# Three queues at the start of a weight-gradient matmul: moving 384 KB from the hardware queues to the software queue

## The chip, the cores and the metric

The kernel runs on one core of a Trainium2 chip. The metric is device time in microseconds (us), the median of several executions. Of one execution the profile gives the span from the first to the last instruction (about 1.8 us less than the device time of the same execution) and a trace of every instruction and every DMA packet. Each kernel has one trace.

## The reference

```python
def setup_inputs():
    batch, m, k, n = 16, 512, 1024, 768
    return {
        "input": np.random.randn(batch, m, k).astype(np.float32),
        "grad_output": np.random.randn(batch, m, n).astype(np.float32),
    }

def reference(input, grad_output):
    return np.einsum('bmk,bmn->kn', input, grad_output).astype(np.float32)
```

Batch and m together are 8192 rows, 64 slices of 128 rows. Each slice has an X part (128 x 1024 float32, 512 KB) and a G part (128 x 768, 384 KB). The result is the sum over slices of X transposed times G.

## The kernel before

TensorE does 12 matmuls of 512 columns for each slice: eight "wide" ones (four in group A, four in group B, X as weights against the 512 wide columns of G) and four "narrow" ones (group N, the 256 narrow columns of G as weights against X). An order, tuned by hand, says which group takes which slice when, so that PSUM's eight banks and the arriving slices suffice:

```python
ORDER = (
    "A1! B1 N1 B2! N2 A2 N3! A3 B3 A4! B5 N5 B6! N7 A6 N8! A9! B10 N9 B12! N12! A12! "
    "B15 AB17! n17! AB26! n26! AB41! n41! AB47 A50! B50! N64!"
).split()
WARMUP = [512] * 10 + [128] * 2
```

"B12!" means: group B goes on up to and including the twelfth slice, then its banks are added to SBUF. Slices are counted from 0 below, so the twelfth is slice 11.

Three queues bring the inputs. GpSimd's software queue casts float32 to bf16 on the way and brings almost everything. The first slices come over the two hardware queues, SP and ACT, as float32, and DVE and ACT round them; TensorE passes the time with matmuls on constants:

```python
    xf = [head.tile([P, K], f32, name=f"xf{s}") for s in range(2)]
    gf = head.tile([P, N], f32, name="gf")
    nc.sync.dma_start(out=gf[:, 0:NA], in_=G[0:P, 0:NA])
    nc.scalar.dma_start(out=xf[0], in_=X[0:P, :])
    nc.sync.dma_start(out=gf[:, NA:N], in_=G[0:P, NA:N])
    nc.scalar.dma_start(out=xf[1], in_=X[P : 2 * P, :])
    # ... warm-up matmuls (L81) ...
    for s in range(1, S):
        gt = xg.tile([P, N], bf16, name="gt")
        nc.gpsimd.dma_start(out=gt, in_=G[s * P : (s + 1) * P, :])
        # ...
        if s > 1:
            xs[s] = xg.tile([P, K], bf16, name="xt")
            nc.gpsimd.dma_start(out=xs[s], in_=X[s * P : (s + 1) * P, :])
    # ...
    round_by("DVE", g0, gf, 0, 256)
    round_by("ACT", g0, gf, 256, NA)
    round_by("DVE", xs[0], xf[0], 0, P)
    round_by("ACT", xs[0], xf[0], 2 * P, 4 * P)
    # ... the rest of X of slice 0
```

## Time and profile before

| | kernel before |
|---|---|
| device time, median of 3 | 175.9 us |
| span of the profiled execution | 174.3 us |
| first real matmul starts | 5.32 us |
| last matmul starts | 171.25 us |
| 768 matmuls of 512 columns at 0.216 us | 165.9 us |
| X of slice 2, the first X of the software queue, lands | 9.70 us |

The lines that carry the argument stand in the prediction below.

### The profile page before, as it was taken

The numbers are of one execution on the slowest core, as the hardware profiler recorded it, in microseconds if no ns is written. First come the engines' busy times: TensorE is split into PE (matmuls) and PEld (weight loads), VectorE is DVE, ScalarE is ACT, GpSimd is POOL, SyncE is SP. The second block draws the span as 40 slices with busy tenths as digits, with TensorE's granted clock in tenths as the row PEclk, the third lists the DMA queues.
The fourth block names the chain that finished last, engine by engine and source line by source line (L and its number), as shares of the span: only waits on it lengthen the run. The fifth ranks groups of instructions, "written<-read, shape, count | busy, mean of one in ns | idle before, by whom it ended". The sixth has DMA issues, their size and how long they took to land.

```text
span 174.3 us, 2013 instructions
## 1 busy us (share of the span) xinstructions
PE 169.9 (97%) x793; PEld 78.4 (45%) x808; DVE 61.3 (35%) x103; ACT 6.2 (4%) x12; POOL 66.7 (38%) x129
## 2 busy tenths in 40 slices
PE   8999999999999999999999999999999999999993
PEld 3444444444444444444444444444444444444463
DVE  0655582883940039300000662200560003931122
ACT  2640000000000000000000000000000000000000
POOL 7444434444444444444444444444274200000000
PEclk9999999999999999999999999999999999999999
DMA  5999999999999999999999999999999990085623
GB/s 192 276 208 209 207 209 208 208 208 209 207 208 209 207 208 210 207 209 209 206 209 208 208 210 207 207 209 208 207 209 209 207 202 11 0 190 160 170 86 120
DMA packets 25048, 33.35 MB, mean 191 GB/s; under 512 B 6480, under 2 KB 16592, under 8 KB 25040
## 3 DMA queue, kind: packets, MB, share of 16 engines
q0 software_dynamic: 18000, 28.65, 89.9%
q10 hardware_dynamic: 4448, 2.10, 4.7%
q1 hardware_dynamic: 2592, 2.49, 4.2%
q8 instruction: 6, 0.10, 0.2%
q14 instruction: 2, 0.02, 0.0%
HBM read 58.72 MB, written 3.15 MB: 355 GB/s over the span
## 4 chain that ended last, share of the span: by engine, by line
PE 97%; issue 0%; DVE 0%
PE bank L127 63%; PE bank L134 32%; PE bank L81 3%; DVE acc L118 0%
## 5 line engine op out<-in xcount | busy, mean ns | idle before, releaser
L127 PE MATMUL bank<-gt,xt 128*128 128x512 bf16 (+2 forms) x515 | 108.3, 367 | 0.5
L127 PEld LDWEIGHTS <-xt 128*128 128x128 bf16 x524 | 50.2, 98 | 57.2
L118 DVE TENSOR_TENSOR acc<-bank,acc 128x512 f32<-128x512 f32 (+2 forms) x62 | 37.9, 667 | 73.4 <-PE bank L127 72.9
L134 PE MATMUL bank<-xt,gt 128*128 128x512 bf16 x242 | 54.8, 379 | 0.3
L97 POOL DMA_DIRECT2D xt<-in_input_dram x62 | 33.1, 533 | 38.7 <-DMA xt<-in_input_dram 36.5
L92 POOL DMA_DIRECT2D gt<-in_grad_output_dram x63 | 33.8, 536 | 31.2 <-DMA gt<-in_grad_output_dram 24.9
L134 PEld LDWEIGHTS <-gt 128*128 128x128 bf16 x252 | 24.6, 98 | 29.7
L118 DVE TENSOR_TENSOR acct<-bank,acct 128x512 f32<-128x512 f32 x24 | 15.7, 682 | 30.0 <-PE bank L134 29.9
L81 PE MATMUL bank<-const-bfloat16-1.0 128*128 128x512 bf16 (+1 forms) x12 | 4.6, 574 | 0.8 <-PEq L263 0.8
L81 PEld LDWEIGHTS <-const-bfloat16-1.0 128*128 128x128 bf16 x12 | 1.6, 140 | 3.5 <-issue 3.5
L122 DVE COPY acc<-bank 128x512 f32<-128x512 f32 x4 | 2.7, 687 | 1.0 <-PE bank L127 1.0
L180 DVE STREAM_TRANSPOSE turned<-acct 128x512 f32<-128x512 f32 x4 | 2.9, 715 | 0.1
L127 PEld LDWEIGHTS <-x 128*128 128x128 bf16 x16 | 1.6, 98 | 1.9 <-DVE x L107 0.2
L107 DVE CAST g<-gf 128x256 bf16<-128x256 f32 x2 | 0.6, 290 | 4.7 <-DMA gf<-in_grad_output_dram 4.7
L124 ACT COPY acc<-bank 128x512 f32<-128x512 f32 x4 | 2.1, 589 | 1.3 <-PE bank L127 1.3
L127 PE MATMUL bank<-gt,x 128*128 128x512 bf16 x8 | 2.1, 379 | 0.0
L127 PE MATMUL bank<-g,x 128*128 128x512 bf16 x8 | 2.0, 398 | 0.0
L122 DVE COPY acct<-bank 128x512 f32<-128x512 f32 x2 | 1.3, 686 | 1.3 <-PE bank L134 1.3
L107 ACT CAST x<-xf 128x256 bf16<-128x256 f32 x4 | 1.4, 409 | 0.0
L107 ACT ACT_TABLE_LOAD x1 | 1.3, 1283 | 1.7 <-PEq L263 1.7
L124 ACT COPY acct<-bank 128x512 f32<-128x512 f32 x2 | 1.1, 588 | 1.5 <-PE bank L134 1.5
L107 DVE CAST x<-xf 128x256 bf16<-128x256 f32 (+1 forms) x5 | 1.0, 260 | 0.0
(8 smaller groups left out, 3.3 us busy)
## 6 DMA issues: line engine op xcount, KB each, us to landing
xt<-in_input_dram POOLq DMA_DIRECT2D x62, 256.0 KB, 8.5
gt<-in_grad_output_dram POOLq DMA_DIRECT2D x63, 192.0 KB, 8.5
out_dram<-acc SPq DMA_DIRECT2D x13, 128.0 KB, 2.7
xf<-in_input_dram ACTq DMA_DIRECT2D x2, 512.0 KB, 5.1
out_dram<-turned ACTq DMA_DIRECT2D x4, 256.0 KB, 3.4
gf<-in_grad_output_dram SPq DMA_DIRECT2D x1, 256.0 KB, 3.9
out_dram<-acc SPq DMA_DIRECT2D x1, 256.0 KB, 2.0
gf<-in_grad_output_dram SPq DMA_DIRECT2D x1, 128.0 KB, 4.7
```

What stands on the lines that cost most here:

```text
L81: nc.tensor.matmul(wps[:, 0:cols], ones, nc.const_aps.tensor(1.0, (P, cols), bf16), start=True, stop=True,)
L92: nc.gpsimd.dma_start(out=gt, in_=G[s * P : (s + 1) * P, :])
L97: nc.gpsimd.dma_start(out=xs[s], in_=X[s * P : (s + 1) * P, :])
L107: copy(out=dst[:, c0:c1], in_=src[:, c0:c1])
L118: nc.vector.tensor_add(out=dst, in0=src, in1=dst)
L122: nc.vector.tensor_copy(out=dst, in_=src)
L124: nc.scalar.copy(out=dst, in_=src)
L127: nc.tensor.matmul(bank, xs[s][:, k * P : (k + 1) * P], gwide[s][:, c0:c1], start=start, stop=stop)
L134: nc.tensor.matmul(bank, gnarrow[s].rearrange("p (r t) -> p t r", t=NT)[:, t], xs[s][:, h * NA : (h + 1) * NA], start=start, stop=stop,)
L180: nc.vector.transpose(out=turned[:, h * hb : (h + 1) * hb, :, t], in_=dst.rearrange("p (b r) -> p b r", r=SQ),)
```

## The change

Its intent: give TensorE its first data sooner. Wide G and the first half of X of slice 0 lead the two hardware queues in equal 2 KB rows, the warm-up is shortened to match, and 384 KB that are needed a little later (narrow G of slice 0, the low half of X of slice 1) go to the software queue, which also saves their rounding.

```diff
-WARMUP = [512] * 10 + [128] * 2
+WARMUP = [512] * 9 + [128] * 3
...
-    nc.sync.dma_start(out=gf[:, 0:NA], in_=G[0:P, 0:NA])
-    nc.scalar.dma_start(out=xf[0], in_=X[0:P, :])
-    nc.sync.dma_start(out=gf[:, NA:N], in_=G[0:P, NA:N])
-    nc.scalar.dma_start(out=xf[1], in_=X[P : 2 * P, :])
+    nc.sync.dma_start(out=gf, in_=G[0:P, 0:NA])
+    nc.scalar.dma_start(out=xf[0][:, 0:NA], in_=X[0:P, 0:NA])
+    nc.sync.dma_start(out=xf[1][:, NA:K], in_=X[P : 2 * P, NA:K])
+    nc.scalar.dma_start(out=xf[0][:, NA:K], in_=X[0:P, NA:K])
...
-    for s in range(1, S):
+    for s in range(S):
...
+        g0 = NA if s == 0 else 0
+        nc.gpsimd.dma_start(out=gt[:, g0:N], in_=G[s * P : (s + 1) * P, g0:N])
+        if s > 0:
+            x1 = NA if s == 1 else K
+            nc.gpsimd.dma_start(out=xs[s][:, 0:x1], in_=X[s * P : (s + 1) * P, 0:x1])
...
-    round_by("DVE", g0, gf, 0, 256)
-    round_by("ACT", g0, gf, 256, NA)
+    round_by("DVE", gwide[0], gf, 0, 304)
+    round_by("ACT", gwide[0], gf, 304, NA)
... (X of slice 0 is rounded in pieces of 128, then 256 columns; narrow G of slice 0
...  and the low half of X of slice 1 are no longer rounded)
-        "N": Part(narrow_mm, [(t, h) for h in range(KH) for t in range(NT)], narrow_dst),
+        "N": Part(narrow_mm, [(t, h) for h in reversed(range(KH)) for t in range(NT)], narrow_dst),
```

More of the change, by code (lines that the diff above doesn't have):

```diff
@@ L70 @@
     xf = [head.tile([P, K], f32, name=f"xf{s}") for s in range(2)]
-    gf = head.tile([P, N], f32, name="gf")
-    nc.sync.dma_start(out=gf[:, 0:NA], in_=G[0:P, 0:NA])
-    nc.scalar.dma_start(out=xf[0], in_=X[0:P, :])
-    nc.sync.dma_start(out=gf[:, NA:N], in_=G[0:P, NA:N])
-    nc.scalar.dma_start(out=xf[1], in_=X[P : 2 * P, :])
+    gf = head.tile([P, NA], f32, name="gf")
+    nc.sync.dma_start(out=gf, in_=G[0:P, 0:NA])
+    nc.scalar.dma_start(out=xf[0][:, 0:NA], in_=X[0:P, 0:NA])
+    nc.sync.dma_start(out=xf[1][:, NA:K], in_=X[P : 2 * P, NA:K])
+    nc.scalar.dma_start(out=xf[0][:, NA:K], in_=X[0:P, NA:K])
     ones = nc.const_aps.tensor(1.0, (P, P), bf16)
@@ L87 @@
         )
-    for s in range(1, S):
-        gt = xg.tile([P, N], bf16, name="gt")
-        nc.gpsimd.dma_start(out=gt, in_=G[s * P : (s + 1) * P, :])
+    for s in range(S):
+        pool = head if s == 0 else xg
+        gt = pool.tile([P, N], bf16, name="gt")
+        pool = head if s < 2 else xg
+        xs[s] = pool.tile([P, K], bf16, name=f"x{s}" if s < 2 else "xt")
         gwide[s] = gt[:, 0:NA]
         gnarrow[s] = gt[:, NA:N]
-        if s > 1:
-            xs[s] = xg.tile([P, K], bf16, name="xt")
-            nc.gpsimd.dma_start(out=xs[s], in_=X[s * P : (s + 1) * P, :])
-    for s in range(2):
-        xs[s] = head.tile([P, K], bf16, name=f"x{s}")
-    g0 = head.tile([P, N], bf16, name="g0")
-    gwide[0] = g0[:, 0:NA]
-    gnarrow[0] = g0[:, NA:N]
+        g0 = NA if s == 0 else 0
[3 more added lines that the diff above has]
+            nc.gpsimd.dma_start(out=xs[s][:, 0:x1], in_=X[s * P : (s + 1) * P, 0:x1])
     def round_by(engine, dst, src, c0, c1):
@@ L107, in round_by @@
         copy(out=dst[:, c0:c1], in_=src[:, c0:c1])
-    round_by("DVE", g0, gf, 0, 256)
-    round_by("ACT", g0, gf, 256, NA)
-    round_by("DVE", xs[0], xf[0], 0, P)
-    round_by("ACT", xs[0], xf[0], 2 * P, 4 * P)
-    round_by("DVE", xs[0], xf[0], P, 2 * P)
-    round_by("DVE", xs[0], xf[0], 4 * P, 6 * P)
-    round_by("ACT", xs[0], xf[0], 6 * P, 8 * P)
+    round_by("DVE", gwide[0], gf, 0, 304)
+    round_by("ACT", gwide[0], gf, 304, NA)
+    for k in range(0, KS // 2, 2):
+        round_by("DVE", xs[0], xf[0], k * P, (k + 1) * P)
+        round_by("ACT", xs[0], xf[0], (k + 1) * P, (k + 2) * P)
+    round_by("DVE", xs[0], xf[0], NA, 6 * P)
+    round_by("ACT", xs[0], xf[0], 6 * P, K)
     def add_out(dst, src):
@@ L172, in add_slice @@
             copy_out(dst, bank, i)
-            if s == 0 and i == 0:
-                round_by("DVE", g0, gf, NA, N)
         else:
@@ L212 @@
     for i, step in enumerate(ORDER):
-        if i == 2:
-            round_by("DVE", xs[1], xf[1], 4 * P, 6 * P)
-            round_by("ACT", xs[1], xf[1], 6 * P, 8 * P)
-            round_by("DVE", xs[1], xf[1], 0, 2 * P)
-            round_by("ACT", xs[1], xf[1], 2 * P, 4 * P)
+        if i == 1:
+            round_by("DVE", xs[1], xf[1], NA, 6 * P)
+            round_by("ACT", xs[1], xf[1], 6 * P, K)
         close = step.endswith("!")
```

## The prediction

> **What bounds the kernel now.** I read the page first, for what the end of the span hangs on.
>
> ```profile
> ## 4 chain that ended last, share of the span: by engine, by line
> PE 97%; issue 0%; DVE 0%
> PE bank L127 63%; PE bank L134 32%; PE bank L81 3%; DVE acc L118 0%
> ```
>
> The chain is TensorE from end to end: wide matmuls (L127), narrow ones (L134), and 3% of warm-up matmuls on constants (L81). No wait holds even 1%. So the time is: when the real matmuls start, plus their number times their spacing, plus every gap in them, plus the tail. There are 64 slices of 12 matmuls of 512 columns, 768 in all. The chain puts groups of four 0.86 us apart, so 0.216 us each and 768 x 0.216 = 165.9 us. The timeline has the first real one at 5.32 and the last addition from PSUM starting at 171.50, which leaves no room for gaps. The change touches neither count nor tail, only the first 5.3 us and the arrivals of early slices. So next I read the timeline of the start (start, duration, then the wait in brackets).
>
> ```profile
> 0.78 4.64 PE L81 MATMUL bank<-const-bfloat16-1.0 128*128 128x512 bf16 x12 [0.78 <-PEq L263]
> ...
> 1.23 1.20 POOL L92 DMA_DIRECT2D gt<-in_grad_output_dram  x2 [0.79 <-POOLq L263]
> ...
> 4.71 0.29 DVE L107 CAST g<-gf 128x256 bf16<-128x256 f32 x1 [4.71 <-DMA gf<-in_grad_output_dram]
> ...
> 5.04 0.56 DVE L107 CAST x<-xf 128x128 bf16<-128x128 f32 x3
> ...
> 5.32 1.55 PEld L127 LDWEIGHTS <-x 128*128 128x128 bf16 x8 [0.17 <-DVE x L107]
> 5.32 2.04 PE L127 MATMUL bank<-g,x 128*128 128x512 bf16 x8
> ```
>
> The reader sees a chain G of slice 0 landed (4.7), X of slice 0 landed (5.0), rounded, first real weights at 5.32, with TensorE waiting 0.17 us for the rounding. The warm-up fills the time until then. Asked over narrow windows, the timeline puts the warm-up matmuls 0.427 us apart, the first real one at 5.32, the second at 5.69 and then one each 0.216: the array ran at half rate until within the first real matmul. Solving 0.362 us = one matmul, part at 0.427 and part at 0.216 per matmul, puts the switch near 5.6. (The granted clock in the page reads full all along; the spacing is the witness.)
>
> Third, the DMA view of two adjoining windows, 4.5 to 5.25 and 5 to 5.5. In the first the software queue has no row at all; in the second it appears:
>
> ```profile
> q10 hardware_dynamic: 64, 0.25, 83.7%
> q1 hardware_dynamic: 69, 0.06, 22.1%
> ...
> q10 hardware_dynamic: 46, 0.19, 94.2%
> q0 software_dynamic: 5, 0.01, 8.4%
> q1 hardware_dynamic: 16, 0.00, 3.6%
> ```
>
> The software queue, first issued at 1.23, moves nothing until about 5.25, when the SP queue (q1) runs dry. From then to 145 us the transfers are saturated at about 208 GB/s. So the third question is how early each slice lands before its first use. I took issue time plus landing time per transfer and set it against the matmul rows. The tightest is X of slice 11:
>
> ```profile
> L97 POOL DMA_DIRECT2D xt<-in_input_dram x1: 530/530/530, 21.0 to 21.0; - x1
> DMA to landing us min/median/max: 9.2/9.2/9.2
> ...
> 29.64 1.89 PE L127 MATMUL bank<-gt,xt 128*128 128x512 bf16 x8
> ```
>
> It lands at about 30.15; the fifth matmul of that row needs it at 29.64 + 4 x 0.216 = 30.50. **Margin about 0.35 us.** Other margins, got likewise: slice 16 0.55, slice 1 0.57, slice 6 0.77, slice 4 0.87, slice 2 0.95; late slices over 1.3. Slice 11 is tight because of an instruction fetch (q8, 16 KB at about 24 us) that occupies one DMA engine for 0.9 us.
>
> **What the Trainium skill says.** "TensorE: Matmul & The Clock Gate", What's actually happening: the array starts at half clock, and a free-running activity window of about 3.4 us decides when it is released, so it is a budget of time and not of matmuls. The 0.427 to 0.216 us step agrees. If so, less warm-up does not bring the switch forward. "DMA: Bandwidth & Descriptors", Queues, rings and completion order: each DMA engine goes round the queues that have work, a packet at a time. Agrees for the two hardware queues: between 3 and 5 us q10 with 4 KB rows moved 0.57 MB and q1 with rows of 2 KB and less 0.25 MB, so the longer row takes the larger share. The same page, Latency and other measured facts, has first byte of a software transfer at about 1 us; this trace has 4 us, and the measurement decides. The same page, SWDGE vs HWDGE vs iDMA: only the software queue casts on the way, so what a hardware queue brings must be rounded by DVE or ACT, as the trace has it.
>
> **The change part by part.**
> 1. *Hardware queues: 1408 KB become 1024 KB, in four transfers of 256 KB.* Wide G and the first half of X of slice 0 lead the two queues, now with equal 2 KB rows, so they share evenly. Summing the DMA windows before, hardware had moved about 150 KB by 2.5 us, 275 by 3.0, then 200 per half us; 512 KB is reached near 3.6 us, or 3.8 if the slow beginning is set by packets and not bytes. Data end to landing was about 0.5 us. Estimate: both land at 4.15 to 4.3, against 4.68 and 5.02. Rounding: 304 columns on DVE, about 0.33 us from the 0.29 us for 256; then 0.2 for 128 columns of X. First weights ready at about 4.85.
> 2. *Warm-up: one 512 becomes one 128.* 0.427 less 0.107 = 0.32 us. The last warm-up matmul ended at 5.21 before (5.10 + 0.107), so now 4.89. Data and warm-up meet at about 4.9, against 5.32: 0.43 us earlier. But if the clock still switches at 5.6, the added time runs at half rate: by 5.6 there are (5.62 - 4.89)/0.427 = 1.7 matmuls done, against 0.7. **Gain 1.0 x 0.216 = 0.2 us**, up to 0.43 if the clock switches earlier.
> 3. *Second half of X of slice 0* is last on its queue, landing near 5.5. Rounded by 5.85; the fifth matmul needs it at about 6.1. Fits, by little.
> 4. *Roundings removed* (narrow G of 0, low half of X of 1): about 0.8 us DVE work and the same on ACT, none of it on the chain. Worth nothing by itself. The narrow groups run high half first, so that X's low half of slice 1 is needed two matmuls later.
> 5. *Software queue: 128 KB of narrow G and 256 KB of X go ahead of slice 2.* Same source bytes as were taken off the hardware queues. Per DMA engine: hardware before 16 packets of 159 ns, 8 of 84, 8 of 46 = 3.58 us; after, 32 of 84 = 2.69, plus 8 of about 59 (1 KB source rows) and 8 of about 97, the last two estimated from the 135 and 173 ns of 1.5 and 2 KB packets: 3.94. So +0.35 us, and up to 0.2 more if hardware is done at 5.1 and software still starts at 5.28. **All slices from 2 on land 0.35 to 0.55 us later.** Narrow G should land near 6.2 (needed 7.0), G of 1 near 7.2 (7.8), X low near 8.0 (9.1), X of 2 at 10.05 to 10.25 (10.4): all just in time.
> 6. *Slice 11*: margin 0.35, less 0.2 for the earlier TensorE, less 0.35 to 0.55 for the later landing: a stall of 0.2 to 0.4 us. That hands back all of the gain.
>
> Sum: -0.2 at the start, +0.2 to +0.4 at slice 11 (and a stall there takes slices 15 and 16 out of danger): 0 to +0.2 us; if the software queue starts as soon as hardware is out, -0.1 to -0.3.
>
> **Rivals.** *The full gain*: 0.32 to 0.43 us, 175.5. It needs the clock released earlier or full rate at once, and no lateness at slice 11. For it: the new split of 304 and 208 columns and the new warm-up look fitted to a measured landing. Against: the arithmetic of the slowest DMA engine. *Arrival binds*: the software stream slips by 0.5 us or more, TensorE waits at slices 2, 4, 6 and 11; since these slacks overlap, the end moves by the largest single deficit only, about +0.3 us, 176.2. For it: margins under 1 us everywhere before 20 us; against: hardware work ends 1.5 us sooner, so software may start sooner. *DVE or ACT becomes the bound at the start* (roundings of X's second half now stand ahead of the copies out of PSUM): DVE free for the first copy at 5.85, second done by 7.25, the narrow matmul that needs that bank at 7.4. If the half lands 0.3 us late, TensorE waits 0.2. *A larger loss* would need TensorE to idle for microseconds, so that the clock drops; nothing here makes a wait that long.
>
> **Range and chances.** The central case between the sum and the fitted look of the change is -0.1: **175.8 us**. The best case is -0.43 (175.47), the worst plausible +0.4 with a further early wait (176.3); repeats of before span 0.16 us. So 175.4 to 176.3. Two per cent is 3.5 us, ten times the largest term either way: faster 0.01, same 0.98, slower 0.01.
>
> **What would show it.** The first real matmul at about 4.9, with one or two at 0.427 spacing before 0.216 (step 2 right); if it starts later than 5.1 step 1 is wrong. Software packets from 5.0 to 5.3 (step 5). A TensorE wait on X of slice 11 near 30 us of 0.2 to 0.4 (step 6); if the matmuls run through from 5 to 171 us, step 5 is wrong and the time is near 175.6. Waits between 6 and 11 us name slice 0's second half or X of 2. What would break the prediction: a software queue that starts much later or earlier than 5.28, or a clock switch that moves.

## More of the kernel before

Executions of the kernel before lie between 175.87 and 176.56 us over four groups of runs, so a difference of a few tenths between single executions says nothing about the time.

One more view is needed later: the DMA engines' work in stretches of half a microsecond. The columns are the stretch, its length, GpSimd's busy time with its number of instructions, the granted clock, the mean busy share of the 16 DMA engines, and GB/s as written. Of the kernel before:

```profile
2.50:3.00 0.50, 0.50 (x2) 1.00 0.80 250
3.00:3.50 0.50, 0.50 (x2) 1.00 1.05 422
...
4.50:5.00 0.50, 0.50 (x2) 1.00 1.05 408
5.00:5.50 0.50, 0.50 (x2) 1.00 1.06 400
5.50:6.00 0.50, 0.22 (x1) 1.00 1.08 308
```

From 3 us on the engines are full. Hardware transfers, written as float32, show as 400 GB/s; the software queue's, written as bf16 at half the bytes, show as 200 GB/s. The fall from 400 to 308 is software taking over.

## The result, and the profile after

The changed kernel takes **176.94 us** (median of 6, 176.86 to 177.37) against 175.97 for the kernel before (6 executions). The ratio is 1.0054, 95% interval 1.0039 to 1.0069: about 0.95 us slower, small but clear, and outside the predicted range. Ratios here are the mean time of one kernel's fast runs over that of the other's fast runs of the same rounds, so they are not quite the ratios of the medians quoted.

The chain that ended last has changed. From the page of the changed kernel:

```profile
PE 94%; DMA 3%; DVE 0%; ACTq 0%; issue 0%
PE bank L126 63%; PE bank L133 32%; DMA xf<-in_input_dram 3%; ACTq L74 0%; DVE x L106 0%; DVE acc L117 0%
```

The warm-up has left the chain and a transfer of X to the float32 tile has entered it. The same chain in order of time (start, duration, what):

```profile
1.18 5.65 DMA xf<-in_input_dram
6.83 0.02 issue
6.86 0.31 DVE x L106
7.16 0.05 issue
7.21 1.04 PE bank L126 x4
```

The transfer issued at 1.18 by ACT is the second half of X of slice 0. It lands at 6.83; DVE rounds it; only then does the fifth real matmul start. The timeline shows what TensorE had done before:

```profile
4.23 0.46 DVE L106 CAST gt<-gf 128x304 bf16<-128x304 f32 x1 [4.23 <-DMA gf<-in_grad_output_dram]
...
4.89 1.06 PE L126 MATMUL bank<-gt,x 128*128 128x512 bf16 x4
...
6.86 0.30 DVE L106 CAST x<-xf 128x256 bf16<-128x256 f32 x1 [1.73 <-DMA xf<-in_input_dram]
...
7.21 1.04 PE L126 MATMUL bank<-gt,x 128*128 128x512 bf16 x4 [1.26 <-DVE x L106]
```

The head did what it was meant to: G landed at 4.2 instead of 4.7, and the first real matmul starts at 4.89 instead of 5.32. The fourth starts at 5.57, against 6.12 before: 0.55 us ahead. But between the fourth and fifth starts lie 1.64 us, where 0.22 is the regular spacing: **a wait of 1.42 us**. (The 1.26 in the bracket is less because the modelled end of a matmul lies after the start of the next.) So 1.42 - 0.55 = 0.87 us lost at the fifth matmul; the last matmul starts at 172.13 instead of 171.25, 0.88 later. There is no other wait in TensorE's stream: that one gap accounts for the profiled loss.

The second finding is in the stream behind it. X of slice 2 was issued at 3.45 and took 7.5 us to land:

```profile
L102 POOL DMA_DIRECT2D xt<-in_input_dram x1: 565/565/565, 3.5 to 3.5; - x1
...
DMA to landing us min/median/max: 7.5/7.5/7.5
```

That is at 10.96 instead of 9.70, and the first slices after it are late by the same amount, 1.2 to 1.3 us. No wait shows, since TensorE is itself late. The DMA engines in the changed kernel, in the stretches shown of before:

```profile
2.50:3.00 0.50, 0.50 (x2) 1.00 0.77 221
3.00:3.50 0.50, 0.50 (x2) 1.00 0.94 356
...
4.50:5.00 0.50, 0.50 (x2) 1.00 0.82 254
5.00:5.50 0.50, 0.50 (x2) 1.00 0.98 222
5.50:6.00 0.50, 0.10 (x1) 1.00 1.13 193
```

Between 4.5 and 5 us they are 0.82 busy and move 254 GB/s where they moved 408. Software has not begun (first packet at 5.21, against 5.28 before: no sooner), and yet hardware's work is not used up: about a quarter of its 1024 KB is still to come. In the trace the rows of each hardware transfer end with 16 packets of 4 bytes, which I take to be one for each DMA engine; for X's second half the first of them comes at 5.21, so by this reading every engine still had rows of it. Why the engines stand partly idle, the trace does not show. From 5.2 on the remainder shares with software. The DMA view of 5.2 to 5.7 (queue, packets, MB, share; q10 is ACT's, q1 SP's, q0 the software queue):

```profile
q0 software_dynamic: 67, 0.04, 54.1%
q10 hardware_dynamic: 37, 0.06, 46.0%
q1 hardware_dynamic: 4, 0.00, 2.3%
```

So there are two candidates for the loss: the one late transfer, and the late stream.

### The profile page after: what moved, and what is told of

Read it like the earlier page. It is cut to its first block, busy times and chain, and to the rows that moved or that the text cites. A ratio compares the mean times of both kernels' runs of the same rounds, so it can differ in the third digit from the quotient of the medians.

```text
span 175.1 us, 2028 instructions
## 1 busy us (share of the span) xinstructions
PE 170.3 (97%) x808; PEld 78.2 (45%) x808; DVE 61.1 (35%) x101; ACT 5.9 (3%) x12; POOL 67.7 (39%) x131
## 4 chain that ended last, share of the span: by engine, by line
PE 94%; DMA 3%; DVE 0%; ACTq 0%; issue 0%
PE bank L126 63%; PE bank L133 32%; DMA xf<-in_input_dram 3%; ACTq L74 0%; DVE x L106 0%; DVE acc L117 0%
## 5 line engine op out<-in xcount | busy, mean ns | idle before, releaser
L99 POOL DMA_DIRECT2D gt<-in_grad_output_dram x64 | 34.3, 535 | 30.8 <-DMA gt<-in_grad_output_dram 24.7
L133 PEld LDWEIGHTS <-gt 128*128 128x128 bf16 x256 | 25.1, 98 | 30.2
L126 PE MATMUL bank<-gt,x 128*128 128x512 bf16 x16 | 4.1, 382 | 1.3 <-DVE x L106 1.3
L133 PE MATMUL bank<-x,gt 128*128 128x512 bf16 x8 | 2.1, 379 | 0.0
L106 DVE CAST gt<-gf 128x304 bf16<-128x304 f32 x1 | 0.5, 458 | 4.2 <-DMA gf<-in_grad_output_dram 4.2
L106 DVE CAST x<-xf 128x128 bf16<-128x128 f32 (+1 forms) x4 | 1.1, 293 | 1.7 <-DMA xf<-in_input_dram 1.7
L106 ACT CAST x<-xf 128x128 bf16<-128x128 f32 (+1 forms) x4 | 1.3, 352 | 1.9 <-DMA xf<-in_input_dram 1.9
```

The lines of the kernel that those rows point to most:

```text
L99: nc.gpsimd.dma_start(out=gt[:, g0:N], in_=G[s * P : (s + 1) * P, g0:N])
L106: copy(out=dst[:, c0:c1], in_=src[:, c0:c1])
L126: nc.tensor.matmul(bank, xs[s][:, k * P : (k + 1) * P], gwide[s][:, c0:c1], start=start, stop=stop)
L133: nc.tensor.matmul(bank, gnarrow[s].rearrange("p (r t) -> p t r", t=NT)[:, t], xs[s][:, h * NA : (h + 1) * NA], start=start, stop=stop,)
```

## The experiments

Twelve kernels ran, each with a correct result, all of them in the fast state but r4_gate, a single look whose state is unknown. Times are medians; the kernel before ran beside each group with medians of 176.13, 176.17 and 176.06. Waits are read from the matmul spacing less 0.22 us, as above.

| kernel | time | ratio, 95% interval | fifth matmul waits | X of slice 2 lands | last matmul starts |
|---|---|---|---|---|---|
| before | 175.9 to 176.2 | | 0 | 9.70 | 171.25 |
| the change | 176.94 | 1.0054, 1.0039 to 1.0069 | 1.42 | 10.96 | 172.13 |
| r1_swap | 176.91 | 1.0032, 1.0011 to 1.0052 | 0.54 | 10.85 | 172.19 |
| r2_whole | 176.56 | 1.0025, 1.0003 to 1.0048 | 0 | 10.70 | 171.53 |
| r3_x1sw | 177.12 | 1.0041, 1.0012 to 1.0070 | 0 | 11.12 | 172.18 |
| r4_gate | 178.91 (one) | | 0 | 12.81 | 174.13 |
| s1_warm | 176.22 | 1.0002, 0.9988 to 1.0016 | 0 | 9.74 | 171.33 |
| s2_split | 177.26 | 1.0058, 1.0045 to 1.0072 | 0 | 10.26 | 172.09 |
| s3_narrow | 176.33 | 1.0010, 0.9996 to 1.0024 | 0 | 9.89 | 171.54 |
| s4_halfx | 176.45 | 1.0011, 0.9998 to 1.0025 | 0 | 10.41 | 171.75 |
| t1_swaporder | 176.57 | 1.0030, 1.0017 to 1.0044 | 0.52 | 10.62 | 171.85 |
| t2_warmorder | 175.92 | 0.9994, 0.9980 to 1.0007 | 0 | 9.89 | 171.49 |
| t3_x1hw | 175.98 | 0.9998, 0.9985 to 1.0011 | 0 | 9.94 | 171.35 |
| t4_afterorder | 176.72 | 1.0037, 1.0024 to 1.0051 | 1.14 | 10.82 | 171.99 |

### Is the wait at the fifth matmul the loss?

**r1_swap** exchanges the two second transfers of the changed kernel.

```diff
-    nc.sync.dma_start(out=xf[1][:, NA:K], in_=X[P : 2 * P, NA:K])
-    nc.scalar.dma_start(out=xf[0][:, NA:K], in_=X[0:P, NA:K])
+    nc.sync.dma_start(out=xf[0][:, NA:K], in_=X[0:P, NA:K])
+    nc.scalar.dma_start(out=xf[1][:, NA:K], in_=X[P : 2 * P, NA:K])
```

> The changed kernel with one exchange: the SP queue's second transfer is the second half of X of slice 0, the ACT queue's second is the high half of X of slice 1. Theory T (the second half of X of slice 0 lands last of the hardware transfers, at 6.83 us, because it is at the tail of the later of two queues, and TensorE waits 1.42 us for it): in the SP place it lands near 6.0, the fifth real matmul starts near 6.4 instead of 7.21, the wait there shrinks to about 0.6 us. But the slices of the software queue, which land 1.25 us later than before, then bind: about 1.0 us at slice 6, so the end moves by about 0.4 us only: about 176.5 us. Rival A (the wait is the whole of the loss): the end follows the fifth matmul fully, 0.8 us, about 176.1. Rival B (the lateness belongs to that data and not to its place): no change, 176.9.

The half landed at 5.69 and the wait fell to 0.54 us. The end did not move: the last matmul starts at 172.19 against 172.13. The chain that ended last, by line, names what took over:

```profile
by line: PE bank L126 53.4%; PE bank L133 27.1%; DMA xt<-in_input_dram 15.0%; POOL gt L99 1.3%; issue 0.7%; POOL x L102 0.3%; POOL xt L102 0.3%; DVE acc L117 0.2%; POOLq L257 0.0%
```

The timeline of TensorE near 31 us shows one of the places:

```profile
30.07 1.03 PE L126 MATMUL bank<-gt,xt 128*128 128x512 bf16 x4
31.44 1.04 PE L126 MATMUL bank<-gt,xt 128*128 128x512 bf16 x4 [0.34 <-DMA xt<-in_input_dram]
```

The chain now runs through the software queue's transfers: TensorE waits 0.15 us at the ninth matmul, 0.3 at slice 2, 0.1 each at slices 4 and 6, and 0.5 at slice 11, whose X lands at 31.39 (30.16 in the kernel before, 30.77 in the change). That one transfer took 9.28 us from issue to landing here, 9.15 in the kernel before and 8.54 in the change; in t4_afterorder below, whose transfers are those of the change, it took 9.22. So how hard slice 11 presses is in part the luck of an execution. So the wait at the fifth matmul is *not* the whole of the loss: ease it and the late stream takes its place. Rival A falls. My 176.5 was low too: I had left slice 11 out of that sum, and slice 6 took 0.1 us and not 1.0. (The interval of the ratio overlaps that of the change; the profile is the firmer witness.)

**r3_x1sw** goes further: all of X of slice 1 on the software queue, SP carries wide G alone.

```diff
-    nc.sync.dma_start(out=xf[1][:, NA:K], in_=X[P : 2 * P, NA:K])
...
-            x1 = NA if s == 1 else K
+            x1 = K
... (the roundings of X of slice 1 go too)
```

> The changed kernel with all of X of slice 1 on the software queue; hardware carries only wide G and X of slice 0, 768 KB. Theory T: with no second transfer on the SP queue, the second half of X of slice 0 lands by 5.5 to 5.8 and the fifth matmul does not wait, or under 0.3 us; but X of slice 1 and all later slices land later still by some 0.2 to 0.6 us, so the end is bound by the software queue: 176.6 to 177.3. Rival A (the wait is the whole loss): 175.5 to 175.7.

With no second transfer on SP, X's second half landed at 5.13 and the first twelve matmuls ran through from 4.65. Then X of slice 1 landed at 8.92 and TensorE waited 1.72 us at the thirteenth. Theory T's range held; the wait merely moved by one slice.

**t4_afterorder** and **t1_swaporder** delay the first use of slice 11 by four matmuls, in the changed kernel and in the exchange.

```diff
-... B10 N9 B12! N12! A12! ...
+... B10 N10 B12! N12! A12! ...
```

> The changed kernel with the step in the order and nothing else. Theory T (in the change itself the wait at the fifth matmul sets the end, slice 11 came in time there): last matmul at 172.1, time 176.9, as the change. Rival (slice 11 sets the end of the change too): 0.3 to 0.5 us faster.

> The exchange of the second hardware transfers (X's second half of slice 0 on SP) with one more step in the order of matmuls: narrow groups of slice 9 go ahead of the wide ones of slice 10, so slice 11 is first used 0.86 us later. In the exchange alone TensorE waited 0.54 us less 0.22 at the fifth matmul, 0.3 at slice 2, and 0.5 at slice 11, and the end was where the change has it. Theory T (two gates in a row: the wait at the fifth matmul, and behind it the late software stream): with both eased the last matmul starts about 0.5 us sooner, 171.7 instead of 172.19, time about 176.4; the wait left is the one at slices 2 to 6. Rival (something later or elsewhere sets the end): 172.2 and 176.9 again.

In t4_afterorder the only wait is again the one at the fifth matmul, which starts 0.14 us sooner than in the change; the last starts 0.14 sooner too. So in the change itself that wait sets the end. The time, 176.72, lies 0.2 under the change's from other runs, within overlapping intervals. In t1_swaporder the wait at slice 11 is gone and the last matmul starts at 171.85, 0.34 us sooner than in the exchange, less than the 0.5 I expected because slice 16 then holds TensorE for 0.26 us. (The expectation takes the 0.22 off the wait at the fifth matmul twice: 0.54 is what is left after it.) The times do not confirm this: the ratios, 1.0030 and 1.0032, are the same, so the 0.34 us is a difference between two traces. The traces show two gates in a row: first the late half of X, behind it the late stream.

### What delays the second half of X?

**r4_gate** holds GpSimd's first transfer until the first half of X has landed (a one-column copy on GpSimd, in program order).

```diff
+    gate = head.tile([P, 1], f32, name="gate")
+    nc.gpsimd.tensor_copy(out=gate, in_=xf[0][:, 0:1])
     for s in range(S):
```

> The changed kernel with GpSimd's first transfer held until the first half of X of slice 0 has landed (a one-column copy of it on GpSimd, about 4.4 us). It tells whether the software queue's 4 us from first issue to first packet are its own, and whether its packets are what delays the second half of X. If the 4 us are its own: first software packet near 8.5, hardware alone until then; if software packets were the cause of the lateness, the second half of X lands by about 5.8, if not, at 6.5 or later. If software merely gave way to the hardware queues: first packet near 5.5. The time itself will be worse, by 1 to 3.5 us, and proves nothing.

The half landed at 5.65 instead of 6.83 (6.69 in t4_afterorder, whose transfers are those of the change), with the same hardware transfers in the same order. DVE rounds it at once:

```profile
5.67 0.29 DVE L108 CAST x<-xf 128x256 bf16<-128x256 f32 x1 [0.88 <-DMA xf<-in_input_dram]
```

So the software queue costs that tail 1.0 to 1.2 us, by one execution with it held back. The stretches of half a microsecond (here with ACT's busy time in the third place) show where:

```profile
4.50:5.00 0.50, 0.45 (x3) 1.00 0.99 377
5.00:5.50 0.50, 0.00 (x0) 1.00 0.10 33
```

With software held back, hardware moves 377 GB/s from 4.5 to 5 and is done. In the change it moved 254 there, in t4_afterorder, r1_swap and t1_swaporder 249 to 285, although no software packet had gone before 4.9 to 5.2. Part of the cost thus comes before the first software packet, part after it, when the two share. What holds the engines in the first part the trace does not show.

The first software packet came at 5.89, 1.38 us after its issue at 4.51, not 4. In the kernel before and in the change software was issued at 1.23 and, by that measure, could have begun near 2.6; it moved nothing until 5.2 to 5.3, while hardware was busy. What lets it start stays open. It is not that SP's queue runs dry, as the prediction read it: in s3_narrow below SP's last packet came at 4.30 and software's first at 5.31, in r3_x1sw at 3.64 and 4.14.

The other competitor is SP's second transfer. In r3_x1sw, without it, the half landed at 5.13 although software began at 4.14 there. Which second transfer gets the engines first shows in the DMA view of 3.7 to 4.3. In the changed kernel SP's (q1) does:

```profile
q1 hardware_dynamic: 91, 0.17, 75.0%
q10 hardware_dynamic: 47, 0.06, 28.6%
```

There the half waits for the high half of X of slice 1, which is needed eight matmuls later, and so falls into the stretch in which software comes in.

### What makes the software stream late?

**r2_whole** puts X of slice 0 back into one transfer of 4 KB rows and leaves the moved bytes moved.

```diff
-    nc.scalar.dma_start(out=xf[0][:, 0:NA], in_=X[0:P, 0:NA])
+    nc.scalar.dma_start(out=xf[0], in_=X[0:P, :])
...
-    nc.scalar.dma_start(out=xf[0][:, NA:K], in_=X[0:P, NA:K])
```

> The changed kernel with X of slice 0 as one transfer of 512 KB in 4 KB rows, as before the change; the bytes given to the software queue stay as in the change. Theory T: X of slice 0 lands near 5.0 as in the kernel before, no wait at the fifth matmul, first real matmul near 5.3. If the late software slices come of the 2 KB rows, X of slice 2 lands near 10.2 and the time is near 176.0; if they come of the 384 KB moved to the software queue, it lands near 10.9, TensorE waits about 0.5 us at slices 4 and 6, and the time is near 176.4. Rival A (wait is the whole loss): about 175.6 to 175.9.

X landed at 5.09, TensorE started at 5.41 and did not wait at the fifth. X of slice 2 still landed at 10.70. So the 2 KB rows are not the main cause of the late stream. TensorE waited 0.1 us each at slices 2, 4 and 6, less than the 0.5 expected. The time, 176.56, lies between those of the kernel before (176.13 beside it) and of the change.

**s3_narrow** and **s4_halfx** add to the kernel before one part of the move each.

```diff
-    nc.sync.dma_start(out=gf[:, NA:N], in_=G[0:P, NA:N])
...
+    nc.gpsimd.dma_start(out=g0[:, NA:N], in_=G[0:P, NA:N])
... (its rounding goes too)
```

> The kernel before with one part of the change: narrow G of slice 0 (128 KB) at the head of the software queue instead of on the SP queue. Theory T (the lateness grows with the bytes moved: 1.0 us for 384 KB in 4 KB rows, so 0.33 us for 128 KB): X of slice 2 lands at 10.0 to 10.1, the wait at slice 11 is about 0, time +0 to +0.2 us. Rival (an extra transfer at the head costs a fixed time): slices 0.7 us or more later, time +0.3 to +0.5.

```diff
-    nc.scalar.dma_start(out=xf[1], in_=X[P : 2 * P, :])
+    nc.scalar.dma_start(out=xf[1][:, NA:K], in_=X[P : 2 * P, NA:K])
...
+        if s == 1:
+            nc.gpsimd.dma_start(out=xs[1][:, 0:NA], in_=X[P : 2 * P, 0:NA])
... (its rounding goes too; narrow groups run high half first, as in the change)
```

> The kernel before with another part of the change alone: the low half of X of slice 1 (256 KB) behind G of slice 1 on the software queue, the high half alone on the ACT queue. Theory T: X of slice 2 lands 0.65 us later, at 10.3 to 10.4; first real matmul stays at 5.3; TensorE waits first at slice 11 and 6, 0.2 to 0.4 us; time +0.2 to +0.4 us. Rival (hardware done sooner lets software start sooner, so nothing is lost): X of slice 2 at 9.7 to 9.9 and the time as before.

With 128 KB moved, X of slice 2 lands at 9.89; with 256 KB at 10.41; with 384 KB at 10.62 to 10.96 (five kernels); with 640 KB (r3_x1sw) at 11.12; with none at 9.70 to 9.89 (before, s1_warm, t2_warmorder). The lateness grows with the bytes moved; for 128 KB alone it is within the spread. One kernel does not fit: s2_split below moved none and has 10.26, with a hardware transfer running beside software until 8.2. So the bytes are the main cause, and not the only one. At slice 11 TensorE waited 0.26 us in s3_narrow (about 0 expected) and 0.51 in s4_halfx (0.2 to 0.4). The times, +0.1% each, are not clear of noise. The rival that hardware, done sooner, would let software start sooner is refuted: software began at 5.31 and 5.37.

In s1_warm, s3_narrow, s4_halfx and r1_swap, where slice 11 is the last wait, the last matmul starts 140.79 to 140.80 us after X of slice 11 lands. In those kernels the arrival of one slice sets the end to a hundredth of a microsecond.

**t3_x1hw** is the test of the whole: the change, but X of slice 1 entirely on SP, so only narrow G stays moved. Two transfers on each hardware queue as before. (The order step is in it too.)

```diff
-    nc.sync.dma_start(out=xf[1][:, NA:K], in_=X[P : 2 * P, NA:K])
+    nc.sync.dma_start(
+        out=xhalves[:, :, 0:NA],          # two padded halves: rows stay 2 KB
+        in_=X[P : 2 * P, :].rearrange("p (h c) -> p h c", c=NA),
+    )
... (GpSimd's part of X of slice 1 goes; its roundings read the two halves)
```

> The changed kernel with all of X of slice 1 on the SP queue (two rows of 2 KB each) instead of its high half, so that only narrow G of slice 0 was moved to the software queue, and with the step in the order. Two transfers for each hardware queue, as in the change. Theory T (the software stream is late by the bytes that were moved to it): X of slice 2 lands at 9.9 to 10.2 against 10.96 in the change; X's second half of slice 0 lands at 5.5 to 6.2, a wait of 0 to 0.5 us at the fifth matmul; time 175.7 to 176.2, half a microsecond or more under the change. Rival (2 KB rows and the early start are what makes it late): X of slice 2 at 10.7 or later, time 176.6 or more.

The time is that of the kernel before, 175.98, ratio 0.9998, and X of slice 2 lands at 9.94. Its timeline of TensorE:

```profile
4.87 1.90 PE L130 MATMUL bank<-gt,x 128*128 128x512 bf16 x8
6.61 1.03 PE L137 MATMUL bank<-x,gt 128*128 128x512 bf16 x4
7.73 1.04 PE L130 MATMUL bank<-gt,x 128*128 128x512 bf16 x4
```

Eight real matmuls from 4.87 without a gap: the half had landed at 5.08. Then 0.25 us are lost at the thirteenth, whose X of slice 1 landed at 7.36, and 0.42 at slice 16; that spends what the early start had won. Theory T holds for the stream. The half came better than T said, and the DMA view of 3.7 to 4.3 tells why:

```profile
q10 hardware_dynamic: 132, 0.24, 103.0%
q1 hardware_dynamic: 9, 0.00, 1.6%
```

Here SP's second transfer, whose two-part pattern took 0.63 us to issue instead of 0.43, had not begun: the nine packets of q1 are 4-byte ones that end its first, and the first row of the second came at 4.58. ACT's half had the engines to itself. Why SP's second came so late, the trace does not show. So this kernel closes both gates at once, the stream by the bytes moved back, the half by its turn. It does not tell what each was worth; the exchange and the delayed order did that.

### The head of the hardware queues alone, and a better version

**s1_warm** shortens only the warm-up of the kernel before.

```diff
-WARMUP = [512] * 10 + [128] * 2
+WARMUP = [512] * 9 + [128] * 3
```

> The kernel before with the shorter warm-up alone (nine of 512 and three of 128 columns). In the kernel before, the first weights wait 0.17 us for rounded data at 5.32 us, so shorter warm-up can bring nothing while the data keep their time. Theory T: first real matmul at 5.3 as before, time the same within 0.1 us. Rival (warm-up sets the start): 0.3 us faster. Rival (the array falls back to half rate without the warm-up): two to three matmuls at 0.427 spacing, 0.3 to 0.6 us slower.

No difference (1.0002). The first real matmul starts at 5.30, when its data are there.

**s2_split** changes only the hardware head of the kernel before: X of slice 0 in two transfers, X of slice 1 as a third on ACT (and, to suit, the warm-up and the roundings).

```diff
-    nc.scalar.dma_start(out=xf[0], in_=X[0:P, :])
+    nc.scalar.dma_start(out=xf[0][:, 0:NA], in_=X[0:P, 0:NA])
+    nc.scalar.dma_start(out=xf[0][:, NA:K], in_=X[0:P, NA:K])
...
     nc.scalar.dma_start(out=xf[1], in_=X[P : 2 * P, :])
```

> The kernel before with only the head of the hardware queues changed: X of slice 0 as two transfers of 256 KB in 2 KB rows on the ACT queue, roundings ordered to suit, shorter warm-up; narrow G of slice 0 and all of X of slice 1 stay on the hardware queues, so the software queue has what it had. Theory T (the loss of the change comes of the 384 KB moved to the software queue and of software packets among the last hardware ones): first real matmul at 4.65 to 4.9, no wait above 0.2 us at the fifth, X of slice 2 lands at 9.7 to 9.9 as before, slice 11 takes back 0.2 to 0.3 us: 175.5 to 175.9 us, at or under the kernel before. Rival (2 KB rows themselves slow the start): X of slice 2 lands after 10.2, a wait at the fifth matmul over 0.5 us, time 176.2 or more.

A clear miss: 177.26, the slowest of those timed. The half landed at 5.67. But ACT's queue then had a hole. The DMA view from 5.2 to 5.7:

```profile
q0 software_dynamic: 67, 0.10, 113.0%
q10 hardware_dynamic: 4, 0.01, 4.0%
```

And from 5.7 to 6.2:

```profile
q10 hardware_dynamic: 29, 0.12, 60.9%
q0 software_dynamic: 36, 0.04, 50.1%
```

The last row of the second transfer came at 5.23. The third, issued at 1.67, sent one packet at 5.58 and the next at 5.78; by then software had the engines, X of slice 1 landed at 8.52 instead of 7.03, and TensorE waited 0.62 us for it. The switch of the array to full rate came late in this execution as well (the first three real matmuls 0.40, 0.43 and 0.34 us apart). So this kernel did not test what it was made for; t3_x1hw, with two transfers to a queue, did. The hole is not peculiar to a third transfer: in t3_x1hw SP's queue stood still from 3.74 to 4.58 between the rows of its first and its second. What makes such a hole is left open.

**t2_warmorder**, s1_warm with the step in the order, was to beat the kernel before.

> The kernel before with the shorter warm-up and the same step in the order. With the shorter warm-up alone, the first matmul started at 5.30 and all eight ran at full rate, but slice 11 took back 0.24 us. Theory T: the wait at slice 11 goes, last matmul starts at 171.1 instead of 171.33, time about 0.2 us under the kernel before, 175.95. Rival (the order costs waits for PSUM banks at the twelfth slices): no gain or a loss of 0.2 us and gaps near 31 to 36 us.

175.92, ratio 0.9994: undecided. The wait at slice 11 is gone and there is no other gap, but in the profiled execution X of slice 0 landed at 5.21 and TensorE started at 5.71, later than in the kernel before. No version here is clearly faster than the kernel before.

## Why the prediction was wrong

The prediction said 175.8, range 175.4 to 176.3, all but surely within 2%. The class was right (ratio 1.0054); the time lies 0.6 us above the range. By its own steps:

- **What bounds it** was right: TensorE from end to end, so every wait before the end adds to the time.
- **Steps 1 and 2** (hardware head and warm-up). Landings at 4.15 to 4.3 were predicted, 4.21 and 4.43 measured; "Data and warm-up meet at about 4.9" and the first matmul started at 4.89. The worth of it was under-stated: 0.55 us at the fourth matmul instead of 0.2. The clock switch did not stay at 5.6. It is not fixed to the program: spacing puts it near 3.9 in r1_swap, near 4.95 in the change, and above 6 in s2_split. So the 0.55 is in part luck of the profiled execution. In r4_gate, with the same start at 4.89, the switch came near 5.7 and the fourth matmul at 5.94, 0.18 ahead, as step 2 has it.
- **Step 3 is the step that failed.** "*Second half of X of slice 0* is last on its queue, landing near 5.5 ... Fits, by little." It landed at 6.83, and 0.31 us of rounding later TensorE went on, 1.42 us late. Its overlap was wrong: I had summed the bytes of hardware as if all 16 engines ended together near 5.1 and software came after. In fact ACT's queue had packets until 6.48, because SP's second transfer took the engines first and the tail then met software; r4_gate, with software held back, had the half at 5.65, r3_x1sw, without SP's second transfer, at 5.13.
- **Step 4** fits what was seen: s3_narrow and s4_halfx save these roundings and are not faster (no run saves them alone). Their size was over-stated: in the trace of before they are two of 0.28 us on DVE and one of 0.41 on ACT, not 0.8 on each.
- **Step 5** had the mechanism right and the size wrong: "All slices from 2 on land 0.35 to 0.55 us later" should have been 1.2 to 1.3. Its sum of 0.35 took packets at their undisturbed length. The packet lists of the two traces, per engine, have hardware at 4.02 us before and 3.37 in the change, and the packets of the 384 KB on the software queue at 1.28: that is +0.64. Another 0.56 are packets of later slices that had already gone when X of slice 2 landed, 92 before and 150 in the change, and small packets are the rest of the 1.26 us. So the term left out is that the engines do not keep step. Those 16 packets of 4 bytes at the end of a transfer show it too: for X's second half they lie between 5.21 and 6.48 in the change, and between 4.94 and 5.29 in r4_gate.
- **Step 6** did not come true in the change: X of slice 11 landed at 30.77, after a quick transfer (8.54 us, 9.15 before, although the instruction fetch that the prediction names, 0.89 us long, is in both traces), and TensorE, already 0.87 late, needed it at 31.38. In the exchange, with the first gate eased, the stall of slice 11 appeared, 0.5 us.
- **The rivals.** *Arrival binds* described the second gate, and sized it 0.3 us where the end was worth 0.9. The third rival had the half of X late by 0.3 us and a wait of 0.2; it was the right transfer, late by 1.3, but TensorE waited for its data and not for a bank.

The lesson of the error is that a margin of 0.25 us ("Rounded by 5.85; the fifth matmul needs it at about 6.1") on the last transfer of two shared queues was taken as a fit. The range should have carried a late half of X with its full consequence.

## What to carry to other kernels

When a transfer leaves one queue for another, ask what shares the engines with the *last* piece that the first wait needs, not when the bytes would be through on average: here half a slice landed 1.3 us after the byte count said. Before easing a wait, list the margins of all later arrivals; in the change X of slice 6 landed 0.38 us and X of slice 11 0.6 us before their first use, so of the 1.42 us of the visible wait less than 0.4 could be won, and in r1_swap, where slice 11 came later, none was. Here the queue that goes on to bring the whole stream, with margins of under a microsecond, was the wrong place for more early bytes.

## What the Trainium skill lacked or had wrong

- "DMA: Bandwidth & Descriptors", Latency and other measured facts, gives a software transfer's first byte at about 1 us. Issued at 4.51, with the last hardware packet at 5.29, it took 1.38 us (r4_gate); issued at 1.23, with both hardware queues busy, 4.0 us, in the kernel before and in the change.
- The same page, Queues, rings and completion order, has each DMA engine take the queues that have work in turn, a packet at a time. For the two hardware queues the trace of the change agrees while both have rows to send: 55 packets of SP to 58 of ACT from 3.0 to 3.6 us, both in 2 KB rows. Software, ready by about 2.6 us if its 1.38 us holds, got no packet until 5.2 us; after that it did share with the rest of ACT's queue (0.04 and 0.06 MB between 5.2 and 5.7 us). The page does not tell of that start.
- The same page, Issuing engines are not separate DMA queues, says that spreading transfers over issuing engines saves only issue time. That speaks of the total, and no run here contradicts it; but the place in a queue counts: here 384 KB moved between queues shifted the arrival of slice 2 by 0.7 to 1.3 us.
- No page that I read tells of a hole between two transfers of one hardware queue that were both issued long before: 5.23 to 5.58 us in s2_split (issued at 1.67), 3.74 to 4.58 in t3_x1hw (issued at 1.19).
- "TensorE: Matmul & The Clock Gate", What's actually happening, has the point of the switch to full rate vary by 500 ns to either side. Between these kernels, whose warm-ups all start at 0.78, it came between about 3.9 and 6.3 us.
